# One FFN's input product in a two-layer FP32 kernel: eight block products per column pair replaced by seven (one level of Strassen's algorithm)

## The chip, the cores and the metric

The kernel runs as one program on one NeuronCore of a Trainium2 chip. Its time is the device time of one execution in microseconds (us). TensorE (PE in the profile) does the matmuls, with its weight loads listed apart as PEld; VectorE (DVE), ScalarE (ACT) and GpSimd (POOL) do elementwise work; SyncE (SP) issues the DMA loads.

## The reference, cut to what matters

Two layers work on 256 latent tokens and 256 context tokens of width 1024. Each layer is a SwiGLU FFN, a mixing part (attention and Fourier branch), and another FFN; the output is a final normalisation of the latent tokens. Everything is FP32.

```
def swiglu(u, w_in, w_out):
    a, b = jnp.split(u @ w_in, 2, axis=-1)
    return (jax.nn.silu(a) * b) @ w_out

def ffn_sublayer(x, m, i, g, w_in, w_out):
    u = modulate(rms_norm(x, g), m, i)
    return x + 0.5 * m[:, 3 * i + 2][:, None] * swiglu(u, w_in, w_out)
```

`w_in` is 1024 x 5632, so `u @ w_in` has 44 column blocks of 128: 22 of `a` and 22 of `b`. The change touches this input product in one place, the first FFN of the second layer (`l = 1`, `f = 0`), which works on both kinds of tokens.

## The kernel before, in words

Activations lie with features on the 128 partitions and tokens along the free dimension: 512 columns, the latent 256 (`LAT`) and then the context 256 (`CTX`). A feature dimension of 1024 is eight blocks `k` of 128. FP32 precision is had from a split: each operand is a rounded high part (type fp32r) and a low part, the difference, and each block product is three matmuls, high x high, high x low and low x high (`mm3`, lines 369 to 375).

Weights come in a fixed order as blocks of 128 x 1024, eight 128 x 128 tiles side by side. The class `Stream` loads them with one SP DMA each (`load_to`, line 176), and `split_pieces` (lines 180 to 194) makes the high part on ACT (line 192) and the low part on DVE or POOL (line 193, which engine is chosen by a pattern, here two on DVE, then one on POOL). `tiles` hands out the pieces and runs loads 6 and splits 2 blocks ahead.

All of this, the normalised input `u` (8 tiles), the gated products `g` (22 tiles, one for each pair) and the weight blocks, lives in one pool `slot` of 46 buffers of 4 KB per partition (line 223). A tile that gets a used buffer waits for the last reader of the tile before it. `tmp` has 7 buffers of 2 KB for short-lived values, and `psum` has 8 banks. Each engine runs its instructions in the order of the program text (`manual_schedule`, line 227); there is no reordering between them.

`ffn` (lines 597 to 673) works in pairs `j` of an `a` column block and the matching `b` block. The first two pairs run step by step with `u` as it becomes ready, latent tokens first (lines 636 to 657). The other twenty pairs run in the loop of lines 663 to 672: 8 blocks `k` x 3 matmuls of 512 columns into bank `pa`, the same into `pb`, and then `gated`: SiLU of `pa` on ACT (line 625), its product with `pb` on DVE (line 626), the high part of `g[j]` on ACT (line 627); `low` (line 631) puts the low part of `g[j]` on DVE.

Then `project_out` (lines 499 to 595) multiplies by `w_out`: for each of eight output blocks `m` it goes through `k = 0` to 21 in that order and needs `g[k]` at step `k`. `modulated` (lines 435 to 453) makes the next `u`; it runs at the end of the FFN before, one token kind after the other. PE does its matmuls in this order and doesn't pass one whose input is missing.

Of the kernel before, what the change touches and what calls it, by code (L numbers as in the profile page):

```python
# [11 lines left out]
F32 = mybir.dt.float32  # L12
# [6 lines left out]
P = 128  # L19
# [63 lines left out]


def ffn_in_order(first):
    order = []
    for k in range(KC):
        for j in range(first):
            order += [(k, j), (k, NF + j)]
    for j in range(first, NF):  # L90
        order += [(k, j) for k in range(KC)]
        order += [(k, NF + j) for k in range(KC)]
    return order
# [68 lines left out]
class Stream:  # L162
# [3 lines left out]
    def __init__(self, nc, pool, blocks):  # L166
        self.nc, self.pool, self.blocks = nc, pool, blocks
        self.raw, self.hl = {}, {}
        self.n_raw = self.n_split = 0
        self.pos = 0  # L170
        self.ahead, self.tick, self.lo_on = (6, 2), None, "v"

# [22 lines left out]

    def split_to(self, b):
        while self.n_split <= min(b, len(self.blocks) - 1):
            for _ in self.split_pieces(1):
                pass
# [20 lines left out]
def tile_kernel(ctx: ExitStack, tc, d, out):  # L220
# [135 lines left out]
    st = Stream(nc, slot, blocks)  # L356

# [5 lines left out]
    def cols(ss):  # L363
        return slice(S * ss[0], S * (ss[-1] + 1))
# [69 lines left out]

    def modulated(u, l, i, s, r):

        c = cols([s])

# [5 lines left out]
        for j in range(KC):  # L444
            t = temp("ut")
            nc.vector.scalar_tensor_tensor(out=t[:, c], in0=x[:, j, c], scalar=mod(l, 3 * i + 1, j, s), in1=r[:, c], op0=ALU.mult, op1=ALU.mult)
            nc.scalar.activation(u[j][:, 0, c], t[:, c], AF.Identity, bias=mod(l, 3 * i, j, s))
            if before:
                low(*before)
            before = j, t  # L450
            if j == KC - 1:
                low(*before)
            yield
# [143 lines left out]
    def ffn(l, f, ss, u, later, after):  # L597
# [34 lines left out]

        first = ffn_first(l, f)
        stagger = [[s] for s in ss] if first == 2 else [ss]
        w = []
        for n, part in enumerate(stagger):
# [5 lines left out]
            for k in range(KC) if first != START_PAIRS else ():  # L642
# [5 lines left out]
                if n == 0 and k == (E_K if e else 4) and later:  # L648
                    later()
                    later = None  # L650
            before = None
# [11 lines left out]
        for j in range(first, NF):  # L663
            pa, pb = bank("pa"), bank("pb")
            for ps in (pa, pb):
                tiles = st.tiles(8)
                for k in range(KC):
                    if len(ss) == 1:
                        mm_wide(ps, tiles[k], u[k], c, k == 0, k == KC - 1)
                    else:  # L670
                        mm3(ps[:, c], tiles[k], parts(u[k], c), k == 0, k == KC - 1)
            low(*gated(j, pa, pb, c))
        return project_out(l, i, ss, lambda k: g[k], NF, after, SILU if f else LN_EXP)
# [683 lines left out]
```

## Time and profile before

| | us |
|---|---|
| median of 3 runs | 2014.0 |
| lowest and highest | 2012.76, 2014.69 |
| the profiled execution: time | 2016.41 |
| its span, first to last instruction | 2014.5 |
| second layer, first FFN: pairs 2 to 21 | 1202.6 to 1420.2 |

In the rows below, a row of the groups of instructions reads "line engine operation output<-inputs, shape out<-in, count | busy time in all, mean ns of one | idle time of that engine just before them". A row of a tile's view gives minimum/median/maximum duration in ns. A row of the timeline reads "start, duration, engine, line, operation". A row of the stretches gives, after the stretch and its length, the busy time (and count) of PE, PEld, DVE, ACT and POOL, then the clock that TensorE was granted (1.00 is full), the DMA share and GB/s. Matmuls overlap in the pipeline, so the time that PE needs for them is read from the distance between starts, not from the duration of one.

### The profile page before, as it was taken

The page shows a single profiled execution, that of the slowest core. Times are in us where ns is not written, and L with a number is a line of the kernel's source. Part 1 is how long each engine was busy: PE and PEld are TensorE (multiplying, and loading weights), DVE is VectorE, ACT ScalarE, POOL GpSimd, SP SyncE. Part 2 cuts the span into 40 slices and gives each one's busy share as a digit, 9 for nine tenths or more (in the row PEclk, how much of TensorE's full clock was granted, in tenths as well). Part 3 has the DMA queues.
Part 4 walks back from the last instruction along what each step waited for, and adds up shares of the span by engine and source line. Part 5 has one row for each costly group of instructions (what it writes and reads, how often), then busy time and mean ns, then how long its engine had stood idle before and what let it go on. Part 6 is the DMA issues. An engine that isn't in the chain of part 4 may idle for free.

```text
span 2014.5 us, 26969 instructions
## 1 busy us (share of the span) xinstructions
PE 1992.3 (99%) x10388; PEld 1702.2 (84%) x10388; DVE 1211.7 (60%) x1832; ACT 823.0 (41%) x1335; POOL 735.6 (37%) x492
## 2 busy tenths in 40 slices
PE   8999999999999999999999999999999999999998
PEld 7888888888888888988888898888888889898887
DVE  5877786667777334677777252332324687776652
ACT  3432232256666323523223242222323565666661
POOL 0334455546553013243358410111222454224463
PEclk9999999999999999999999999999999999999999
DMA  9555565413222334455569332222421333555461
GB/s 378 204 169 176 167 210 210 165 58 110 92 85 93 105 105 137 157 172 173 178 212 353 104 131 82 91 74 84 139 91 53 126 128 119 192 172 193 158 203 59
DMA packets 86704, 297.58 MB, mean 148 GB/s; under 512 B 10032, under 2 KB 13232, under 8 KB 86576
## 3 DMA queue, kind: packets, MB, share of 16 engines
q1 hardware_dynamic: 86288, 295.34, 43.7%
q8 instruction: 81, 1.33, 0.3%
q10 hardware_dynamic: 288, 0.52, 0.1%
q14 instruction: 47, 0.39, 0.1%
HBM read 287.44 MB, written 1.05 MB: 143 GB/s over the span
## 4 chain that ended last, share of the span: by engine, by line
PE 93%; DVE 3%; ACT 2%; issue 1%; POOL 1%; DVEq 0%; POOLq 0%; ACTq 0%
PE po L375 7%; PE po L374 7%; PE po L373 7%; PE pa L373 5%; PE pb L375 5%; PE pa L375 5%; PE pb L373 5%; PE pa L374 5%; PE pb L374 5%; PE pg L373 2%; PE pg L375 2%; PE pg L374 2%; PE po L380 2%; PE pb L380 2%; PE pa L380 2%; PE pv L696 1%
## 5 line engine op out<-in xcount | busy, mean ns | idle before, releaser
L193 POOL TENSOR_TENSOR wlo<-wraw,whi 128x1024 fp32r<-128x1024 f32 x139 | 366.0, 2635 | 605.4 <-ACT whi L192 487.1
L192 ACT ACTIVATE whi<-wraw 128x1024 fp32r<-128x1024 f32 x392 | 395.5, 1049 | 74.8 <-PE po L374 34.1
L193 DVE TENSOR_TENSOR wlo<-wraw,whi 128x1024 fp32r<-128x1024 f32 x253 | 350.3, 1394 | 117.9 <-ACT whi L192 116.3
L302 DVE SCALAR_TENSOR_TENSOR junk<-mraw,cond 128x1024 bf16<-128x1024 f32 x224 | 303.1, 1395 | 1.1 <-DMA mraw<-in_w_mod 1.1
L373 PE MATMUL po<-g,whi 128*128 128x512 f32 (+1 forms) x616 | 223.8, 363 | 0.0
L375 PE MATMUL po<-g,wlo 128*128 128x512 f32 (+1 forms) x616 | 223.3, 362 | 0.0
L374 PE MATMUL po<-g,whi 128*128 128x512 f32 (+1 forms) x616 | 223.3, 362 | 0.0
L627 ACT ACTIVATE g<-gv 128x512 fp32r<-128x512 f32 (+1 forms) x92 | 51.7, 562 | 373.6 <-DVE gv L626 344.0
L317 POOL TENSOR_SCALAR mval<-macc,small 128x2 f32<-128x2 f32 (+1 forms) x88 | 122.3, 1394 | 216.2 <-DVE junk L302 216.2
L373 PE MATMUL pa<-u,whi 128*128 128x512 f32 x472 | 183.6, 389 | 0.0
L374 PE MATMUL pa<-u,whi 128*128 128x512 f32 x472 | 183.6, 389 | 0.0
L375 PE MATMUL pa<-u,wlo 128*128 128x512 f32 x472 | 183.6, 389 | 0.0
L373 PE MATMUL pb<-u,whi 128*128 128x512 f32 x472 | 183.6, 389 | 0.0
L374 PE MATMUL pb<-u,whi 128*128 128x512 f32 x472 | 183.6, 389 | 0.0
L375 PE MATMUL pb<-u,wlo 128*128 128x512 f32 x472 | 183.6, 389 | 0.0
L626 DVE TENSOR_TENSOR gv<-silu,pb 128x512 f32<-128x512 f32 x59 | 40.6, 688 | 182.3 <-PE pb L375 181.3
L462 DVE SCALAR_TENSOR_TENSOR x<-po,mval,x 128x256 f32<-128x256 f32 x73 | 32.6, 479 | 194.5 <-PE po L375 194.5
L374 PEld LDWEIGHTS po<-g,whi 128*128 128x128 f32 x616 | 116.3, 189 | 18.3
L373 PEld LDWEIGHTS po<-g,whi 128*128 128x128 f32 x616 | 116.2, 189 | 18.3
L375 PEld LDWEIGHTS po<-g,wlo 128*128 128x128 f32 x616 | 116.2, 189 | 17.9
L424 POOL TENSOR_TENSOR acc<-acc,sq 128x256 f32<-128x256 f32 (+1 forms) x46 | 53.2, 1156 | 191.5 <-ACT sq L413 191.5
L413 ACT ACTIVATE sq<-x 128x256 f32<-128x256 f32 (+1 forms) x48 | 24.7, 516 | 235.3 <-DVE x L462 202.8
(262 smaller groups left out, 4555.2 us busy)
## 6 DMA issues: line engine op xcount, KB each, us to landing
wraw<-in_ffn_in SPq DMA_DIRECT2D x176, 512.0 KB, 4.2
mraw<-in_w_mod SPq DMA_DIRECT2D x128, 512.0 KB, 3.7
wraw<-in_ffn_out SPq DMA_DIRECT2D x88, 512.0 KB, 4.4
wraw<-in_qk SPq DMA_DIRECT2D x32, 512.0 KB, 4.0
wraw<-in_g SPq DMA_DIRECT2D x32, 512.0 KB, 4.4
mfirst<-in_w_mod_first SPq DMA_DIRECT2D x16, 512.0 KB, 10.2
wraw<-in_v SPq DMA_DIRECT2D x16, 512.0 KB, 4.1
wraw<-in_attn SPq DMA_DIRECT2D x16, 512.0 KB, 4.0
```

The lines of the kernel that those rows point to most:

```text
L192: nc.scalar.activation(hi[:, c], raw[:, c], AF.Copy)
L193: eng.tensor_tensor(out=lo[:, c], in0=raw[:, c], in1=hi[:, c].bitcast(F32), op=ALU.subtract)
L302: nc.vector.scalar_tensor_tensor(out=tmp.tile([P, D], BF16, tag="t", name="junk"), in0=mod_raw[n], scalar=1.0, in1=cond[s], op0=ALU.mult, ...
L317: eng.tensor_scalar(out=o, in0=v, scalar1=b_mod[:, b:b + 1], scalar2=0.5 if i % 3 == 2 else 1.0, op0=ALU.add, op1=ALU.mult)
L373: nc.tensor.matmul(ps, hi, uh, start=first, stop=False)
L374: nc.tensor.matmul(ps, hi, ul, start=False, stop=False)
L375: nc.tensor.matmul(ps, lo, uh, start=False, stop=last)
L380: nc.tensor.matmul(ps.rearrange("p (a b) -> p a b", a=2), hi, t[:, :, c], start=first, stop=False)
L424: nc.gpsimd.tensor_tensor(out=self.acc[:, c], in0=self.acc[:, c], in1=sq[:, c], op=ALU.add)
L462: nc.vector.scalar_tensor_tensor(out=x[:, m, c], in0=ps[:, c], scalar=mod(l, 3 * i + 2, m, s), in1=x[:, m, c], op0=ALU.mult, op1=ALU.add)
L626: nc.vector.tensor_tensor(out=v[:, c], in0=sl[:, c], in1=pb[:, c], op=ALU.mult)
L627: nc.scalar.activation(g[j][:, 0, c], v[:, c], AF.Copy)
```

## The change

For pairs 4 to 21 of this one FFN the product of a pair is seen as a 2 x 2 by 2 x 2 block product: rows `a` and `b`, inner blocks `k` 0 to 3 and 4 to 7, columns latent and context. It is done with seven block products of 4 x 3 matmuls of 256 columns, where the eight of the plain form were done as 16 x 3 matmuls of 512. The seven need sums of weight blocks (`s1`, `s2`) and of input blocks (`tq`), and sums of the results.

- The packing order of the weights puts the four quarters of a pair into two blocks, `r0` and `r1`. These blocks are loaded, but not split, by `Stream` (`whole`, `take`).
- `modulated` also writes an unsplit copy of `u` (`full`, four slots) with one more ACT operation for each `k` and token kind.
- `sums` makes the four combinations of input blocks for one quarter index and splits them into two `tq` slots; it runs four times, twice during the first two pairs and twice in pair 2.
- `prepare` makes the seven split weight operands of a pair. It is a generator with five steps, run between the products of the pair before. `sevens` hands on the five steps of its first pair one by one, and yields again only at its own end.
- The gated products of pairs 10 to 21 are kept unsplit, two to a slot (`gf`), and split after the last pair.

```diff
-def ffn_in_order(first):
+SEVEN = {(1, 0): (4, 10)}
...
+    low, high = range(KC // 2), range(KC // 2, KC)
+    for j in range(seven, NF):
+        order += [(k, j) for k in low] + [(k, NF + j) for k in high]
+        order += [(k, NF + j) for k in low] + [(k, j) for k in high]
...
             nc.scalar.activation(u[j][:, 0, c], t[:, c], AF.Identity, bias=mod(l, 3 * i, j, s))
+            if keep:
+                q = j % (KC // 2)
+                if q not in full:
+                    full[q] = slot.tile([P, 4, S], F32, tag="s", name="uf")
+                nc.scalar.activation(full[q][:, 2 * (j // (KC // 2)) + s], t[:, c], AF.Identity, bias=mod(l, 3 * i, j, s))
...
+        def sums(q):
...
+            b = full.pop(q)
+            nc.vector.tensor_tensor(out=b[:, 0], in0=b[:, 0], in1=b[:, 1], op=ALU.subtract)
...
+            tq[q] = [slot.tile([P, 4, S], F32R, tag="s", name="tq") for _ in range(2)]
+            nc.scalar.activation(tq[q][0], b, AF.Copy)
+            nc.vector.tensor_tensor(out=tq[q][1], in0=b, in1=tq[q][0].bitcast(F32), op=ALU.subtract)
+
+        def sevens(j0, held_from):
...
+            def prepare(j, w):
...
+                r0, r1 = (st.take(block(j) + n) for n in range(2))
+                h0, l0 = (slot.tile([P, 1024], F32R, tag="s", name=n) for n in ("h0", "l0"))
+                nc.scalar.activation(h0, r0, AF.Copy)
+                s1 = slot.tile([P, 1024], F32, tag="s", name="s1")
+                for n in (one, two):
+                    nc.vector.tensor_tensor(out=s1[:, n], in0=r0[:, n], in1=r1[:, one], op=ALU.add)
+                nc.gpsimd.tensor_tensor(out=l0, in0=r0, in1=h0.bitcast(F32), op=ALU.subtract)
+                w["a11"], w["a22"] = ((h0[:, n], l0[:, n]) for n in (one, two))
+                yield
+                s2 = slot.tile([P, 1024], F32, tag="s", name="s2")
+                nc.vector.tensor_tensor(out=s2[:, one], in0=s1[:, two], in1=r0[:, one], op=ALU.add)
+                nc.vector.tensor_tensor(out=s2[:, two], in0=s2[:, one], in1=r1[:, two], op=ALU.add)
...
+                yield
+                a12 = slot.tile([P, 1024], F32R, tag="s", name="a12")
+                nc.scalar.activation(a12[:, one], r1[:, two], AF.Copy)
+                nc.vector.tensor_tensor(out=a12[:, two], in0=r1[:, two], in1=a12[:, one].bitcast(F32), op=ALU.subtract)
...
+                yield
...
+                nc.scalar.activation(h1, s1, AF.Copy)
+                nc.gpsimd.tensor_tensor(out=l1, in0=s1, in1=h1.bitcast(F32), op=ALU.subtract)
...
+                yield
...
+                nc.scalar.activation(h2, s2, AF.Copy)
+                nc.vector.tensor_tensor(out=l2, in0=s2, in1=h2.bitcast(F32), op=ALU.subtract)
...
+                yield
...
+            def result(j, v, sl):
+
+                nc.vector.tensor_tensor(out=v[:, :S], in0=ps2[j][:, :S], in1=v[:, :S], op=ALU.subtract)
+                ps2.pop(j)
+                if j < held_from:
+                    nc.vector.tensor_tensor(out=v, in0=sl, in1=v, op=ALU.mult)
+                    return
...
+                g[j] = held.pop(0)
+                nc.vector.tensor_tensor(out=g[j], in0=sl, in1=v, op=ALU.mult)
...
+            for _ in prepare(j0, ws[j0]):
+                yield
...
+            for j in range(j0, NF):
...
+                p1, ps2[j], p3 = bank("pone"), bank("ptwo"), bank("pthree")
+                v, sl = temp("gv"), temp("silu")
+                some(todo, 1)
+                product(p1, w, "a11", b11, True)
+                nc.scalar.activation(v[:, :S], p1[:, :S], AF.Copy)
+                some(todo, 1)
+                product(p3, w, "s1", t1, True)
+                nc.scalar.activation(v[:, S:], p3[:, :S], AF.Copy)
+                nc.gpsimd.tensor_tensor(out=v[:, S:], in0=v[:, S:], in1=v[:, :S], op=ALU.add)
+                some(todo, 1)
+                if before:
+                    i, vi, si = before
+                    product(ps2[i], ws.pop(i), "a22", t4, False)
+                    result(i, vi, si)
+                some(todo, 1)
+                product(ps2[j], w, "s2", t2, True)
+                nc.vector.tensor_tensor(out=sl[:, S:], in0=ps2[j][:, :S], in1=v[:, S:], op=ALU.subtract)
+                if before and i < held_from:
+                    parted(i, vi)
+                some(todo, 1)
+                product(p1, w, "a12", b21, False)
+                nc.scalar.activation(sl[:, :S], p1[:, :S], AF.Silu)
+                if before and i < held_from:
+                    low(g[i], slice(0, 512), vi)
+                product(p3, w, "s4", b22, False)
+                nc.vector.tensor_tensor(out=sl[:, S:], in0=p3[:, :S], in1=sl[:, S:], op=ALU.subtract)
+                nc.scalar.activation(sl[:, S:], sl[:, S:], AF.Silu)
+                st.load_to(block(j + 2) + 1)
+                product(ps2[j], w, "s3", t3, False)
+                nc.vector.tensor_tensor(out=v[:, S:], in0=ps2[j][:, :S], in1=v[:, S:], op=ALU.subtract)
+                before = j, v, sl
+                del p1, p3
+            st.split_to(st.pos + 1)
+            i, vi, si = before
+            product(ps2[i], ws.pop(i), "a22", t4, False)
+            result(i, vi, si)
+            tq.clear()
+            st.load_to(st.pos + 3)
+            for j in range(held_from, NF):
+                v = g[j]
+                parted(j, v)
+                low(g[j], slice(0, 512), v)
+            yield
...
-        for j in range(first, NF):
+        seven, held_from = SEVEN.get((l, f), (NF, NF))
+        more = sevens(seven, held_from) if seven < NF else iter(())
+        for j in range(first, seven):
...
+                if full:
+                    sums(min(full))
+                elif seven < NF:
+                    some(more, 3)
             low(*gated(j, pa, pb, c))
+        some(more, 100)
```

`product` is 4 x 3 matmuls of 256 columns, `parted` is the ACT copy that makes the high part of `g[j]`, `some(steps, n)` advances a generator `n` times, and `t1` to `t4` are the four quarters of the `tq` tiles.

More of the change, by code (lines that the diff above doesn't have):

```diff
@@ L79, with ffn_in_order @@
 STEPWISE = [[0, 3, 3, 1], [4, 2]]
-def ffn_in_order(first):
+SEVEN = {(1, 0): (4, 10)}
+def ffn_in_order(first, seven=NF):
     order = []
@@ L171, in __init__ @@
         self.ahead, self.tick, self.lo_on = (6, 2), None, "v"
+        self.whole, self.n_whole = set(), {}
     def load_to(self, b):
@@ L194, in split_pieces, with take @@
             yield
+    def take(self, b):
+        self.load_to(b)
+        return self.raw.pop(b)
     def split_to(self, b):
         while self.n_split <= min(b, len(self.blocks) - 1):
+            if self.n_split in self.whole:
+                self.n_split += 1
+                continue
             for _ in self.split_pieces(1):
@@ L356, in tile_kernel @@
     st = Stream(nc, slot, blocks)
+    per_layer = len(blocks) // DEPTH
+    for (l, f), (j, _) in SEVEN.items():
+        b = l * per_layer + (per_layer - 66 if f else 0)
+        st.whole |= set(range(b + 2 * j, b + 2 * NF))
+        st.n_whole[l, f] = b + 2 * j
     def tick():
@@ L433, in total @@
             return rsqrt(ps, D, c, "rinv")
+    full = {}
     def modulated(u, l, i, s, r):
         c = cols([s])
+        keep = i != 1 and (l, i // 2) in SEVEN
         def low(j, t):
@@ L650, in ffn @@
                     later = None
+                if n and k in (3, 7) and full:
+                    sums(min(full))
             before = None
@@ L662, in ffn @@
                 nc.scalar.activation(cond[n], cond[n], AF.Silu)
-        for j in range(first, NF):
+        seven, held_from = SEVEN.get((l, f), (NF, NF))
+        more = sevens(seven, held_from) if seven < NF else iter(())
+        for j in range(first, seven):
             pa, pb = bank("pa"), bank("pb")
-            for ps in (pa, pb):
+            for n, ps in enumerate((pa, pb)):
                 tiles = st.tiles(8)
@@ L671, in ffn @@
                         mm3(ps[:, c], tiles[k], parts(u[k], c), k == 0, k == KC - 1)
+                if full:
+                    sums(min(full))
+                elif seven < NF:
+                    some(more, 3)
             low(*gated(j, pa, pb, c))
+        some(more, 100)
         return project_out(l, i, ss, lambda k: g[k], NF, after, SILU if f else LN_EXP)
@@ L1335 @@
         for f in range(2):
[L1336 removed]
+            dr[f"ffn_in_{l}{f}"] = pack(a["ffn_w_in"][l, f], ffn_in_order(ffn_first(l, f), SEVEN.get((l, f), (NF,))[0]))
             dr[f"ffn_out_{l}{f}"] = pack(a["ffn_w_out"][l, f], FFN_OUT_ORDER)
```

48 lines of the change are left out of this document (47 added, 1 removed).

## The prediction

> **What bounds the kernel now.** I read the page first, then the busy time by stretches around the FFN that changes, then the durations of its groups, then single collisions in the timeline.
>
> ```profile
> span 2014.5 us, 26969 instructions
> PE 1992.3 (99%) x10388; PEld 1702.2 (84%) x10388; DVE 1211.7 (60%) x1832; ACT 823.0 (41%) x1335; POOL 735.6 (37%) x492
> ...
> PE 93%; DVE 3%; ACT 2%; issue 1%; POOL 1%; DVEq 0%; POOLq 0%; ACTq 0%
> ...
> 1203.00:1420.00 217.00, 217.00 (x959) 179.64 (x959) 67.97 (x68) 62.65 (x82) 31.79 (x13) 1.00 0.28 86
> 1420.00:1435.00 15.00, 15.00 (x68) 12.43 (x67) 7.36 (x4) 7.61 (x8) 5.37 (x2) 1.00 0.48 161
> ```
>
> PE is the bound. In the stretch of pairs 2 to 21, and at the start of `project_out` behind it, it has no idle time at full clock, while DVE works 68 of 217 us, ACT 63 and POOL 32. Fewer matmuls would pay here if nothing else fills up.
>
> ```profile
> L373 PE MATMUL pa<-u,whi x160: 389/389/396, 1202.6 to 1414.1; 128*128 128x512 f32 x160
> L375 PE MATMUL pb<-u,wlo x160: 389/389/389, 1208.5 to 1420.0; 128*128 128x512 f32 x160
> ...
> 1193.23 0.28 PE L373 MATMUL pf<-u,whi 128*128 128x256 f32 x1
> 1202.23 0.28 PE L373 MATMUL pf<-u,whi 128*128 128x256 f32 x1
> ```
>
> From 1202.6 to 1420.0 are 959 steps between 960 matmuls of 512 columns: 0.2267 us each. Between the two `pf` rows lie 75 steps of 256 columns: 0.120 us each, more than half of 0.2267. A pair costs 48 x 0.2267 = 10.88 us.
>
> **The change, term by term.**
>
> *PE.* A pair becomes 84 matmuls of 256 columns: 84 x 0.120 = 10.08 us, 0.80 us less. Eighteen pairs: **-14.4 us**, if PE stays the bound. The Trainium skill ("TensorE: Matmul & The Clock Gate", section "Back-to-back issue gap") gives N/2.4 + 2.5 ns for N columns, 216 and 109 ns; by it a pair would save 1.2 us and the change 21 us. The trace shows 11 ns more for both sizes, and the measurement decides.
>
> *Elementwise work.* In these pairs a weight block took one ACT copy and one subtraction; now sums, four splits, result sums and a longer way to `g` are needed.
>
> ```profile
> L193 DVE TENSOR_TENSOR wlo<-wraw,whi x23: 1216/1226/2630, 1216.1 to 1391.1; 128x1024 fp32r<-128x1024 f32 x23
> L193 POOL TENSOR_TENSOR wlo<-wraw,whi x11: 2394/2403/2537, 1227.1 to 1390.2; 128x1024 fp32r<-128x1024 f32 x11
> ...
> L192 ACT ACTIVATE whi<-wraw 128x1024 fp32r<-128x1024 f32 x40 | 39.8, 1044 | 0.0
> L631 DVE TENSOR_TENSOR g<-gv,g 128x512 fp32r<-128x512 f32 x19 | 13.2, 693 | 13.5 <-ACT g L627 13.5
> L627 ACT ACTIVATE g<-gv 128x512 fp32r<-128x512 f32 x19 | 12.0, 632 | 106.9 <-DVE gv L626 106.9
> ...
> L951 POOL TENSOR_TENSOR osqp<-osq,osqp 128x256 fp32r<-128x256 f32 x5 | 3.7, 736 | 0.4
> ...
> L386 DVE TENSOR_TENSOR silu<-pa,silu x20: 423/425/427, 1840.7 to 1940.9; 128x256 f32<-128x256 f32 x20
> ...
> L622 DVE TENSOR_TENSOR gv<-silu,gv x20: 425/910/966, 1842.3 to 1943.4; 128x256 f32<-128x256 f32 x20
> ...
> 1248.74 2.36 DVE L193 TENSOR_TENSOR wlo<-wraw,whi 128x1024 fp32r<-128x1024 f32 x2 [0.26 <-ACT whi L192]
> ```
>
> Two DVE operations back to back take 2.36 us, not 2 x 1.22: each overlaps the next by 0.08. So a subtraction of 1024 columns occupies DVE for 1.14 us, one of 512 for 0.61, one of 256 from PSUM for 0.34. A new pair has on DVE: two `s1`, two `s2`, the low part of `a12`, the product in `result` and `low`, seven of 512 with both inputs in SBUF (4.29), `l2` of 1024 (1.14), and four of 256 that read PSUM (1.38): **6.81 us**. POOL gets `l0` and `l1` (2.40 each) and one addition of 256 (0.74). ACT gets three copies of 1024, two of 512 and four of 256, about 6 us. Each alone fits under 10.08 us.
>
> *They don't run side by side.* This is what I weigh most:
>
> ```profile
> 1227.05 2.40 POOL L193 TENSOR_TENSOR wlo<-wraw,whi 128x1024 fp32r<-128x1024 f32 x1 [18.40 <-ACT whi L192]
> 1227.96 2.58 DVE L193 TENSOR_TENSOR wlo<-wraw,whi 128x1024 fp32r<-128x1024 f32 x1 [1.21 <-ACT whi L192]
> ...
> 1840.46 2.49 POOL L193 TENSOR_TENSOR wlo<-wraw,whi 128x1024 fp32r<-128x1024 f32 x1 [4.74 <-ACT whi L192]
> 1840.68 0.42 DVE L386 TENSOR_TENSOR silu<-pa,silu 128x256 f32<-128x256 f32 x1
> 1842.32 0.92 DVE L622 TENSOR_TENSOR gv<-silu,gv 128x256 f32<-128x256 f32 x1
> ```
>
> The DVE subtraction at 1227.96 takes 2.58 us for 1.23 us of work: it began at 1229.31, 0.14 before POOL's ended at 1229.45. At 1840 the operation that reads PSUM (`pa`) isn't slowed under POOL (0.42), the one with both inputs in SBUF is (0.92; 0.910 in the median, against 0.425 for the same size undisturbed). So a POOL operation and a DVE operation with two SBUF inputs exclude each other, each for its whole length, with a handover of 0.14. The Trainium skill says so ("SBUF — State Buffer", section "Who interferes with whom": the shared pair is an exclusive lock, and a DVE instruction with two SBUF inputs contends with a GpSimd one that reads SBUF); the trace agrees with 0.910 against 0.425. It is the rule that speaks against this change.
>
> A POOL turn costs DVE 2.40 - 0.14 = 2.26 us, the small one 0.60. Per pair the two engines then need 4.29 + 1.14 + 2 x 2.26 + 0.60 = **10.55 us** if one of them always holds the lock: a floor above PE's 10.08. The order of the program doesn't reach it. DVE's queue for a pair is: `s1`, `s1`, `s2`, `s2`, `a12` low, `result` (two), `sl`, `l2`, `low`, `sl`, `v`. POOL's `l0`, addition and `l1` become ready (ACT copies `h0`, `p3`, `h1`) while DVE is in the first four, so all three turns fall between DVE operations that wait for them, and the PSUM readers, which could run under POOL, stand behind in the queue. That makes 6.81 + 5.12 = 11.9 us. For pairs whose predecessor is below 10, `l2` also waits: it needs `h2` on ACT, which stands behind `parted`, which waits for the product in `result`: after that 0.54 + 1.04 + some 0.15 of handover, of which DVE fills 0.34 with `sl`. So 13.3 us. Without `parted` and `low` it is 11.9 - 0.6 + about 0.2 = 11.5.
>
> PE feels it at its seventh product (`s3`): it accumulates into the bank that DVE's first `sl` must have read, so PE idles there for what is over 10.08, 1.4 to 3.2 us each pair. PE can't get ahead, since the operands of the next pair come from the same queue.
>
> Six pairs (5 to 10) at 13.3 and twelve at 11.5 are 218 us. Slots: `u` 8, `tq` 8, `g` 10 and up to 5 `gf` leave 15 of 46, and a pair in flight uses up to 15. From about pair 16 on a tile waits for the last reader of one that has just come free: between 0 and 2 us for each of six pairs; I take 1. Loop: **224 us** against 18 x 10.88 = 195.8: **+28 us** (ends: 190 at the floor of 10.55, 240 if all pairs take 13.3).
>
> *The end of the loop.* In pair 3 the generator is advanced three times behind `pa` and three times behind `pb`. `prepare` gives five steps; the sixth call runs through the whole loop of eighteen pairs to the last `yield`. `gated` of pair 3 stands behind that call, so its SiLU, product, copy and `low` come behind the twelve `parted` and `low` of the held pairs on ACT and DVE. `project_out` needs `g[3]` at its fourth step, 3 x 0.68 = 2.0 us after it starts. DVE by then has, from PE's last product: 0.2 to arrive, 0.34 + 0.61, twelve times 0.61 = 7.3, then 0.69 + 0.63 + 0.69 and handovers: 10.7 us. PE stands for about **9 us** where it had no idle time before. A stall of that length also lowers the clock:
>
> ```profile
> 12.00:15.00 3.00, 1.25 (x9) 0.85 (x7) 1.95 (x3) 2.42 (x3) 0.00 (x0) 1.00 1.07 391
> 15.00:18.00 3.00, 2.70 (x15) 2.70 (x16) 2.86 (x4) 0.00 (x0) 0.00 (x0) 0.67 1.03 410
> ...
> 1173.00:1203.00 30.00, 29.69 (x240) 29.14 (x240) 21.12 (x41) 17.31 (x33) 3.20 (x2) 1.00 0.54 207
> ...
> L447 ACT ACTIVATE u<-ut,mval x16: 492/510/512, 1174.9 to 1195.4; 128x256 fp32r<-128x256 f32 x16
> ```
>
> A stretch in which PE worked 1.25 of 3 us is followed by one at 0.67, some 3.4 us at half clock: **+1.5 us**. Later steps of `project_out` are covered: `low` runs ahead of them.
>
> *Before the loop.* Sixteen more ACT copies of 0.51 us stand between those that the context products wait for (PE waited some 0.3 us there); four `sums` (DVE 2.5 us, ACT 1.0 each) lie beside pair 2's 10.9 us. Cover is nearly all there: 0 to 2 us, I take **+1**. The `tq` split and the raw loads, two blocks for each pair as before, hide under PE.
>
> *Sum:* 28 + 9 + 1.5 + 1 = +39.5. The profiled execution took 2016.4 (2 us around its span of 2014.5), the median is 2014.0; I add to the median: **2054 us**.
>
> **The rivals.**
>
> - *The lock packs.* DVE and POOL drift until one always holds it: 10.55 to 11 us a pair, the loop 190 to 198. With 11.5 for the ends: 2014 - 6 + 11.5 to 2014 + 2 + 11.5, so 2018 to 2038 with what lies between. For: the floor itself. Against: three POOL turns that DVE's order can't use.
> - *PE stays the bound, the end stalls:* -14.4 + 11.5 = -3, 2011 us. It needs collisions to be absorbed; the 20 rows of `L622` speak against it.
> - *PE stays the bound and the end doesn't stall* (the other side): `g[3]` finished before the held pairs, or the sums' collisions without price: 2014 - 14.4 + 1 = 2001 us. It decides if DVE and POOL together stay under 10.08 a pair.
> - *Worse:* every pair at 13.3, slots short: 240 + ends, 2070 us.
> - That the change doesn't do what it says: then PE's count would not rise by 18 x (84 - 48) = 648.
>
> **How the numbers follow.** Forecast, 2038 to 2070: 0.66. Packed, 2018 to 2038: 0.17. End stall alone, about 2011: 0.08. Faster, about 2001: 0.09. A measurement of this kernel can tell some 0.2%, 4 us, from no change. So faster 0.09, same 0.08, slower 0.83. Range: 2020 to 2070, leaving out the two cases at or below 2014 and the tail above.
>
> **What would show it.** In the profile after: PE count 11036; starts of the first products 11.5 to 13.3 us apart, with PE idle before the seventh product and DVE's first `sl` as its releaser; `s2` and the low part of `a12` with means far over 0.69 us; one PE wait of some 9 us before the fourth step of `project_out` with `low` (L631) as releaser, then a clock below 1. I am wrong if DVE's two-input operations show undisturbed means, if pairs stand 10.1 us apart, or if `g` of pair 3 is done before the held ones.

## The result, and the profile after

The changed kernel takes **2063.7 us** in the median (2061.77 to 2067.32, four runs), beside 2013.64 us for the kernel before on the same chip (2012.76 to 2014.69, four runs). The ratio is 1.025, with a 95% interval of 1.0233 to 1.0268: 2.5% slower, 50 us. The profiled execution took 2065.36 us, with a span of 2063.6.

One line of the diff above is miscopied: in the loop, the first `sl` line stands with `in1=v[:, S:]`. The program (line 789 after) has `in1=v[:, :S]`, so this instruction waits for ScalarE's copy of `p1` and not for GpSimd's addition. Line numbers from here on are those of the changed kernel: `wlo` is on L203, `prepare` on L692 to 725 (`s1` L699, `s2` L704 and 705, the low part of `a12` L710), the loop on L767 to 804. In the experiments a line can stand a few further down.

The head of the page and its chain, then the stretches (the columns are as before: busy time and count of PE, PEld, DVE, ACT and POOL, granted clock, DMA share, GB/s) around the changed loop and at the start of `project_out`:

```profile
span 2063.6 us, 28653 instructions
PE 1994.5 (97%) x11036; PEld 1733.2 (84%) x11036; DVE 1375.7 (67%) x2008; ACT 873.9 (42%) x1445; POOL 821.2 (40%) x534
PE 82%; DVE 12%; ACT 3%; issue 2%; POOL 1%; DMA 1%; SPq 0%; DVEq 0%; ACTq 0%; POOLq 0%
```

```profile
1225.00:1435.00 210.00, 176.97 (x1342) 171.63 (x1341) 192.03 (x189) 87.58 (x140) 109.28 (x50) 0.94 0.23 72
1465.00:1480.00 15.00, 8.28 (x25) 6.37 (x26) 12.55 (x13) 9.94 (x13) 5.29 (x2) 0.66 0.58 217
```

PE's count rose by 648, so the change does what it says, and PE's busy time is nearly what it was (1994.5 against 1992.3): the time was not spent in matmuls. In the loop PE works 177 of 210 us where it worked all of them, DVE 192. Over the whole chain DVE's share went from 3% to 12%. In which instructions, the groups of DVE and POOL in the loop tell (x18 is once a pair; mean ns behind the busy time):

```profile
L710 DVE TENSOR_TENSOR a<-wraw,a 128x512 fp32r<-128x512 f32 x18 | 47.5, 2637 | 0.0
L704 DVE TENSOR_TENSOR s<-s,wraw 128x512 f32<-128x512 f32 x18 | 39.6, 2200 | 0.8
L699 DVE TENSOR_TENSOR s<-wraw 128x512 f32<-128x512 f32 x36 | 34.2, 990 | 2.9 <-DMA wraw<-in_ffn_in 2.8
L722 DVE TENSOR_TENSOR l<-s,h 128x1024 fp32r<-128x1024 f32 x18 | 24.1, 1338 | 8.0 <-ACT h L721 8.0
L705 DVE TENSOR_TENSOR s<-s,wraw 128x512 f32<-128x512 f32 x18 | 19.7, 1097 | 0.6
L754 DVE TENSOR_TENSOR gf<-silu,gv 128x512 f32<-128x512 f32 x12 | 10.1, 838 | 0.5
...
L789 DVE TENSOR_TENSOR silu<-ptwo,gv 128x256 f32<-128x256 f32 x18 | 7.5, 417 | 0.3 <-PE ptwo L734 0.3
```

```profile
L732 PE MATMUL ptwo<-tq,h 128*128 128x256 f32 x216 | 65.3, 302 | 30.1 <-DVE silu L789 29.5 <-DVE gv L802 0.6
```

A subtraction of 512 columns takes 0.69 us undisturbed; here L710 takes 2.64 and L704 2.20 in the mean, while L789, which reads PSUM, keeps its 0.42. PE waits 29.5 us for that L789, at the seventh product. The timeline of one pair shows why L704 and L710 are long: each lasts until a POOL operation ends.

```profile
1250.19 2.82 POOL L700 TENSOR_TENSOR l<-wraw,h 128x1024 fp32r<-128x1024 f32 x1 [3.84 <-ACT h L696]
1252.98 1.18 POOL L781 TENSOR_TENSOR gv<-gv 128x256 f32<-128x256 f32 x1
1254.13 2.85 POOL L716 TENSOR_TENSOR l<-s,h 128x1024 fp32r<-128x1024 f32 x1
```

```profile
1250.77 2.79 DVE L704 TENSOR_TENSOR s<-s,wraw 128x512 f32<-128x512 f32 x1
1253.60 1.12 DVE L705 TENSOR_TENSOR s<-s,wraw 128x512 f32<-128x512 f32 x1
1254.63 2.89 DVE L710 TENSOR_TENSOR a<-wraw,a 128x512 fp32r<-128x512 f32 x1
```

POOL's `l0` ends at 1253.01 and L704 at 1253.56, 0.55 us later; POOL's `l1` ends at 1256.98 and L710 at 1257.52. Between the two, POOL's addition and L705 take their turns in the same way.

And in `project_out`, the wait at its fourth step, with the clock that follows (a matmul of 512 columns every 0.43 us where it was 0.23):

```profile
1471.72 0.79 PE L396 MATMUL po<-g,whi 128*128 128x512 f32 x1 [8.12 <-ACT g L658]
...
1473.04 0.63 PE L398 MATMUL po<-g,wlo 128*128 128x512 f32 x1
1473.46 0.63 PE L396 MATMUL po<-g,whi 128*128 128x512 f32 x1
1473.89 0.63 PE L397 MATMUL po<-g,whi 128*128 128x512 f32 x1
```

Comparing the starts of the same matmuls in the two profiled executions gives the account of the 49.1 us between the spans:

| where | us |
|---|---|
| in the program's first 31 us, in which both kernels do the same | +1.9 |
| from there to the first pair of seven (its start at 1224.38 becomes 1230.29, 5.9 later in all) | +4.0 |
| loop of 18 pairs: 195.84 becomes 231.08 | +35.2 |
| start of `project_out` to a point late in its eighth block, behind the norm's first two matmuls: 115.75 becomes 126.70 | +11.0 |
| given back behind it, nearly all in the last FFN | -3.0 |

### The profile page after: what moved, and what is told of

Its sections match the earlier page's. It is cut to its first block, busy times and chain, and to the rows that moved or that the text cites. A ratio compares the mean times of both kernels' runs of the same rounds, so it can differ in the third digit from the quotient of the medians.

```text
span 2063.6 us, 28653 instructions
## 1 busy us (share of the span) xinstructions
PE 1994.5 (97%) x11036; PEld 1733.2 (84%) x11036; DVE 1375.7 (67%) x2008; ACT 873.9 (42%) x1445; POOL 821.2 (40%) x534
## 4 chain that ended last, share of the span: by engine, by line
PE 82%; DVE 12%; ACT 3%; issue 2%; POOL 1%; DMA 1%; SPq 0%; DVEq 0%; ACTq 0%; POOLq 0%
PE po L396 7%; PE po L398 7%; PE po L397 7%; PE pa L396 3%; PE pb L396 3%; PE pa L397 3%; PE pb L397 3%; PE pa L398 3%; PE pb L398 3%; DVE a L710 2%; PE pg L396 2%; PE pg L397 2%; PE pg L398 2%; DVE s L704 2%; PE po L403 2%
## 5 line engine op out<-in xcount | busy, mean ns | idle before, releaser
L203 POOL TENSOR_TENSOR wlo<-wraw,whi 128x1024 fp32r<-128x1024 f32 x127 | 337.6, 2660 | 455.5 <-ACT whi L202 380.7
L202 ACT ACTIVATE whi<-wraw 128x1024 fp32r<-128x1024 f32 x356 | 359.6, 1049 | 74.7 <-PE po L397 29.7
L203 DVE TENSOR_TENSOR wlo<-wraw,whi 128x1024 fp32r<-128x1024 f32 x229 | 313.9, 1379 | 108.1 <-ACT whi L202 104.2
L658 ACT ACTIVATE g<-gv 128x512 fp32r<-128x512 f32 (+1 forms) x74 | 40.4, 545 | 269.2 <-DVE gv L657 237.5
L398 PE MATMUL pb<-u,wlo 128*128 128x512 f32 x328 | 127.7, 389 | 0.6 <-POOL wlo L203 0.6
L398 PE MATMUL pa<-u,wlo 128*128 128x512 f32 x328 | 127.7, 389 | 0.5 <-DVE wlo L203 0.5
L396 PE MATMUL pa<-u,whi 128*128 128x512 f32 x328 | 127.7, 389 | 0.0
L397 PE MATMUL pa<-u,whi 128*128 128x512 f32 x328 | 127.6, 389 | 0.0
L397 PE MATMUL pb<-u,whi 128*128 128x512 f32 x328 | 127.6, 389 | 0.0
L396 PE MATMUL pb<-u,whi 128*128 128x512 f32 x328 | 127.6, 389 | 0.0
L732 PE MATMUL ptwo<-tq,h 128*128 128x256 f32 x216 | 65.3, 302 | 30.1 <-DVE silu L789 29.5
```

The lines of the kernel that those rows point to most:

```text
L202: nc.scalar.activation(hi[:, c], raw[:, c], AF.Copy)
L203: eng.tensor_tensor(out=lo[:, c], in0=raw[:, c], in1=hi[:, c].bitcast(F32), op=ALU.subtract)
L396: nc.tensor.matmul(ps, hi, uh, start=first, stop=False)
L397: nc.tensor.matmul(ps, hi, ul, start=False, stop=False)
L398: nc.tensor.matmul(ps, lo, uh, start=False, stop=last)
L732: nc.tensor.matmul(ps[:, :S], hi[:, k], bh, start=first and q == 0, stop=False, skip_group_check=True)
```

## The experiments

The theory was that of the prediction: turns of POOL and DVE at the memory make a pair 11.5 to 13.3 us long, `gated` of pair 3 stalls the projection, and, seen in the trace after, DVE comes into the loop with a backlog. The rival to the first: the pairs are long because of the order of DVE's queue, the slots or the waits for POOL's results, whatever the memory does.

**The gate ahead of the loop.**

```diff
-                    some(more, 3)
+                    some(more, 3 - n)
```

> Only the last step's call is cut from three steps to two where it is made the second time (`some(more, 3 - n)`), so that the gate of pair 3 is issued ahead of the loop and not behind it; nothing else is moved. My theory of the end (the gate of pair 3 stands behind the twelve held pieces, and TensorE waits 8.51 us for it at the fourth step of the projection): that wait goes, and with it the lower clock behind it; 10.95 us were measured from the start of the projection to its m = 7, so the time falls by 8 to 11 us, to 2053 to 2056. Rival (the projection is late because the slots and the held pieces are late, whatever the gate does): the wait moves to a later step of the projection, and the time stays at 2061 or more. The loop itself keeps its 231 us by both, give or take 2.

Measured: 2060.81 us (ratio to before 1.0238, 1.0223 to 1.0253), 3 us less, where 8 to 11 were expected: it lies between the two ranges, just under the rival's. By the ratios it is 2.4 us less, with intervals that overlap, so what the edit did is read from the traces. The wait of 8.12 us is gone, as the same stretch of `project_out` shows, which here has full clock. A shorter one stands later in that stretch, for a weight's low part that GpSimd makes:

```profile
1465.00:1480.00 15.00, 13.00 (x58) 10.47 (x58) 11.30 (x17) 12.57 (x18) 8.38 (x2) 1.00 0.77 286
...
1478.59 0.50 PE L398 MATMUL po<-g,wlo 128*128 128x512 f32 x1 [2.00 <-POOL wlo L203]
```

That is the rival's kind of move, at a quarter of the size. From its start to the same point in the eighth block the projection takes 118.10 us, 8.6 less. But the loop takes 235.93, 4.85 more, against "give or take 2". Of that 1.6 us come in the first eight pairs, where the gate now stands ahead of the first pair's parts on DVE, and 3.2 in pairs 16 to 20. A gate made before the loop holds a slot all through it, and the loop was short of slots at its end already; a late transfer moves DVE's operations against POOL's turns:

```profile
1389.61 4.04 DVE L699 TENSOR_TENSOR s<-wraw 128x512 f32<-128x512 f32 x2 [1.29 <-DMA wraw<-in_ffn_in]
```

So the mechanism of the end is as predicted, and removing it moved some of the cost elsewhere. That a slot is the reason is argued here; the runs on held pairs below bear on it.

**GpSimd's three operations on VectorE.**

```diff
-                nc.gpsimd.tensor_tensor(out=l0, in0=r0, in1=h0.bitcast(F32), op=ALU.subtract)
+                nc.vector.tensor_tensor(out=l0, in0=r0, in1=h0.bitcast(F32), op=ALU.subtract)
...
-                nc.gpsimd.tensor_tensor(out=l1, in0=s1, in1=h1.bitcast(F32), op=ALU.subtract)
+                nc.vector.tensor_tensor(out=l1, in0=s1, in1=h1.bitcast(F32), op=ALU.subtract)
...
-                nc.gpsimd.tensor_tensor(out=v[:, S:], in0=v[:, S:], in1=v[:, :S], op=ALU.add)
+                nc.vector.tensor_tensor(out=v[:, S:], in0=v[:, S:], in1=v[:, :S], op=ALU.add)
```

> The three operations that GpSimd has in a pair (`l0`, `l1` and the addition in `v`) are given to VectorE; the order of each queue, the slots and the products stay. My theory (GpSimd and VectorE take turns at the memory that they share, so that GpSimd's time comes on top of VectorE's): VectorE then has 6.81 + 2 x 1.15 + 0.32 = 9.43 us in a pair, less than the 10.08 us of the products; the pairs stand 10.1 to 11 us apart in place of 11.7 to 14.5, the loop takes 190 to 200 us in place of 231, and the total is 2020 to 2034 with the wait at the end still there. Rival (the pair is long because VectorE's own queue is long or because its order holds it, and GpSimd's work lies beside it): VectorE gets 2.6 us more in every pair and the loop gets longer, by up to 17 x 2.6 = 44 us, for 2064 to 2108.

Measured: 2024.6 us (1.0058, 1.0043 to 1.0073), 39 us less than the change, with *more* work on the busiest elementwise engine. The rival's range begins 39 us higher. The groups of DVE, and a stretch of the loop:

```profile
L704 DVE TENSOR_TENSOR s<-s,wraw 128x512 f32<-128x512 f32 x18 | 12.3, 686 | 0.0
L710 DVE TENSOR_TENSOR a<-wraw,a 128x512 fp32r<-128x512 f32 x18 | 12.3, 685 | 0.0
```

```profile
1244.00:1375.00 131.00, 131.00 (x1092) 130.81 (x1091) 120.98 (x188) 67.19 (x111) 0.00 (x0) 1.00 0.31 97
```

L704 and L710 are back at 0.69 us, PE has no idle time from 1244 to 1375, and twelve pairs in a row stand 10.08 us apart, which is the prediction's 84 x 0.120. DVE is busy 121 of 131 us and that suffices. The loop takes 189.8 us; the wait in the projection is still there, 8.20 us.

**Turns, or waits for results?** The first run gives GpSimd reads whose results nobody uses, the second writes alone; both start from the kernel with everything on VectorE.

```diff
+    spare = const.tile([P, 384], BF16, name="spare")
...
+                for n in (slice(0, 384), slice(384, 768)):
+                    nc.gpsimd.tensor_tensor(out=spare, in0=r0[:, n], in1=h0[:, n].bitcast(F32), op=ALU.subtract)
...
+                for n in (slice(0, 384), slice(384, 768)):
+                    nc.gpsimd.tensor_tensor(out=spare, in0=s1[:, n], in1=h1[:, n].bitcast(F32), op=ALU.subtract)
...
+                nc.gpsimd.tensor_tensor(out=spare[:, :S], in0=v[:, S:], in1=v[:, :S], op=ALU.add)
                 nc.vector.tensor_tensor(out=v[:, S:], in0=v[:, S:], in1=v[:, :S], op=ALU.add)
```

> VectorE keeps all of a pair's work, as in the run without GpSimd (2024.6 us), and GpSimd gets five operations a pair at the old places whose results nobody reads: four subtractions 128x384 of `r0`, `h0` and of `s1`, `h1`, and the addition of the halves of `v`, written to a spare tile. So no product and no other operation waits for a result of GpSimd, while it reads two operands again. My theory (turns at the memory): some 4 x 0.9 + 0.6 = 4.2 us of GpSimd's turns come on top of VectorE's 5.43 + 2.62 = 8.05 us with two operands in SBUF, with the handovers 12.9 us a pair at least: the pairs stand 12.9 to 14.5 us apart and the total is 2072 to 2100. Rival (the loop was long because work waited for GpSimd's results, which take 2.9 us each, and not because of turns): nothing waits for them now, so the pairs stay at 10.1 and the total is 2020 to 2030.

Measured: 2082.1 us (one run), inside the theory's range, 57 us over the kernel without GpSimd and even over the change. From the second on, pairs stand 12.65 to 14.40 us apart. DVE's operations are long again (three lines stand ahead of them, so L707 is the first `s2` and L713 the low part of `a12`): against their means without GpSimd they take 58 us more in the loop. One wait for GpSimd was left in after all (the addition in place must wait until GpSimd has read `v`), 7.5 us over the loop, far too little for 57:

```profile
L707 DVE TENSOR_TENSOR s<-s,wraw 128x512 f32<-128x512 f32 x18 | 24.4, 1353 | 0.0
L713 DVE TENSOR_TENSOR a<-wraw,a 128x512 fp32r<-128x512 f32 x18 | 23.8, 1322 | 0.0
...
L787 DVE TENSOR_TENSOR gv<-gv 128x256 f32<-128x256 f32 x18 | 15.8, 877 | 7.5 <-POOL spare L786 7.5
```

```diff
                 nc.vector.tensor_tensor(out=s2[:, two], in0=s2[:, one], in1=r1[:, two], op=ALU.add)
+                nc.gpsimd.memset(r0, 0.0)
...
+                nc.gpsimd.memset(r1, 0.0)
...
+                nc.gpsimd.memset(s1, 0.0)
...
+                nc.gpsimd.memset(s2, 0.0)
```

> As the run without GpSimd (2024.6 us), and GpSimd clears `r0`, `r1`, `s1` and `s2` in each pair behind their last reader (four memsets of 128 x 1024, some 1 us each by the nearest row, 64x512 in 0.52 us): it only writes. The Trainium skill, page SBUF - State Buffer, section Who interferes with whom, says that a VectorE instruction with two operands in SBUF contends with a GpSimd instruction that reads SBUF, not with one that only writes it. By that rule the pairs stay at 10.1 to 10.6 us and the total is 2022 to 2034. Rival (any work of GpSimd takes the turn): 4.2 us of turns come on top, the pairs stand 12.5 to 14 us apart, total 2065 to 2095.

Measured: 2032.88 us (one run). GpSimd is busy 68.7 us in the loop, and DVE doesn't feel it:

```profile
L706 POOL MEMSET wraw<- 128x1024 f32 x18 | 17.2, 956 | 77.6 <-DVE s L704 60.4 <-ACT h L717 9.1 <-ACT a L710 8.1
```

```profile
L699 DVE TENSOR_TENSOR s<-wraw 128x512 f32<-128x512 f32 x36 | 23.2, 686 | 9.8 <-DMA wraw<-in_ffn_in 9.8
...
L704 DVE TENSOR_TENSOR s<-s,wraw 128x512 f32<-128x512 f32 x18 | 12.3, 686 | 0.0
L711 DVE TENSOR_TENSOR a<-wraw,a 128x512 fp32r<-128x512 f32 x18 | 12.3, 685 | 0.0
```

The means are 0.686 and 0.685 us, to the nanosecond those without GpSimd. The rule of the Trainium skill ("SBUF — State Buffer", section "Who interferes with whom": a VectorE instruction with two SBUF inputs contends with a GpSimd instruction that reads SBUF, not with one that only writes it) agrees with these two runs. Of the 8 us over the run without GpSimd 5.8 stand in the loop, nearly all of them late, where pairs stretch to 10.5 to 14.3 us and DVE waits 9.8 us for transfers instead of 5.3. That a buffer is free only when GpSimd has cleared it is the likely reason; it is argued. Another 3.0 us stand in the last FFN, which the edit doesn't touch (see the last section).

**Start later.** With the gate ahead of the loop, and GpSimd as in the change:

```diff
-SEVEN = {(1, 0): (4, 10)}
+SEVEN = {(1, 0): (6, 10)}
...
-                    some(more, 3)
+                    some(more, 3 if (j, n) == (3, 0) else 2 if (j, n) == (3, 1) else 0)
```

> The seven products begin two pairs later (`SEVEN` (6, 10)), and the gate of pair 3 is issued ahead of the loop as in the run before last: pairs 4 and 5 are made with eight products, in which VectorE can work off the four `sums` that stood ahead of the first pair's parts. My theory of the start (the first pair's parts are late because VectorE comes with a backlog: 18.55 us for the first pair in place of some 11.7, and three to four us ahead of it): the first pair of seven is then 11.5 to 13 us long and the start comes without a wait; two pairs with eight products cost 10.9 us each in place of 12 to 14. So 7 to 12 us less than with the gate alone: 2042 to 2049. Rival (the first pair is long whatever comes before, since its parts are made in line and not one pair ahead): the first pair stays at 17 us or more and the time is within 4 us of that with the gate alone, 2049 to 2056.

Measured: 2054.06 us (1.0203, 1.0188 to 1.0219), 6.75 less than with the gate alone. The time is above the range given and inside the rival's, since both stood on a gate that saves 10; the gain is just short of the 7 to 12 expected. The first pair takes 13.53 us in place of 21.57, where the rival said 17 or more. But the edit did two things: it put two plain pairs behind the `sums`, and it had the first pair's parts made two pairs ahead of their use and no longer just before it. So it doesn't tell a backlog on DVE from parts made in line. For the backlog speak the plain pairs, which were late too: PE waits 3.06 us for a weight split on DVE there.

**All three together.** The two lines of the run just shown, and the three operations on VectorE.

```diff
-SEVEN = {(1, 0): (4, 10)}
+SEVEN = {(1, 0): (6, 10)}
...
-                nc.gpsimd.tensor_tensor(out=l0, in0=r0, in1=h0.bitcast(F32), op=ALU.subtract)
+                nc.vector.tensor_tensor(out=l0, in0=r0, in1=h0.bitcast(F32), op=ALU.subtract)
...
-                    some(more, 3)
+                    some(more, 3 if (j, n) == (3, 0) else 2 if (j, n) == (3, 1) else 0)
```

> All three edits together: GpSimd's operations on VectorE, the gate ahead of the loop, the first pair of seven two pairs later. My theory (turns at the memory, backlog at the start, gate at the end, and nothing else of size): 14 or 15 pairs at 10.1 to 10.5 us where the kernel before has 10.88, no stall at the end, so that the loop with its two plain pairs takes 188 to 196 us against the 195.8 of before, and the total is 2004 to 2016 against 2013.6: from 0.5% faster to the same. Rival (a fourth term that all three leave in place, the slots or ScalarE's share): 2020 or more.

Measured: 2016.92 us (1.0022, 1.0013 to 1.0032): just over the theory's range, below the rival's. The trace names three rests: four of the last five distances are 11.07 to 11.53 us, PE waits 2.06 us for a weight split on GpSimd early in the projection, and pairs 3 to 5 take some 5 us more than 10.88 each, with PE waiting for weight splits that come late behind the `sums`.

**Backlog mended, fewer pairs held.**

```diff
-SEVEN = {(1, 0): (6, 10)}
+SEVEN = {(1, 0): (6, 14)}
...
-            nc.vector.tensor_tensor(out=tq[q][1], in0=b, in1=tq[q][0].bitcast(F32), op=ALU.subtract)
+            late.append((q, b))
+            while late and (late[0][0] != q or not full):
+                p, b = late.pop(0)
+                nc.vector.tensor_tensor(out=tq[p][1], in0=b, in1=tq[p][0].bitcast(F32), op=ALU.subtract)
...
-                    some(more, 3 if (j, n) == (3, 0) else 2 if (j, n) == (3, 1) else 0)
+                    some(more, 3 if (j, n) == (4, 0) else 2 if (j, n) == (4, 1) else 0)
```

> As the run with all three edits (2016.92 us), with three more: pairs 6 to 13 are split as they come and 14 to 21 held (`SEVEN` (6, 14), where 10 and on were held), the parts of the first pair of seven are prepared in the halves of pair 4 and not of pair 3, and in `sums` the low part of one quarter is issued behind the subtractions of the next, so that VectorE doesn't wait 1.13 us for ScalarE in each. My theory: of the run with all three, the last five pairs were 1 to 1.5 us over 10.08 for want of slots (about 5 us), the projection began with 2.45 us of waiting, and pairs 3 and 4 lost some 5 us to VectorE's backlog; most of the first two and about half of the third go, so 2006 to 2012, that is 0.1 to 0.3% faster than the kernel before. Rival (VectorE at 9.43 us a pair and 0.68 more for each pair that isn't held is itself the bound): the pairs up to 13 slip by 0.3 to 1 us each and the time stays at 2014 to 2020.

Measured: 2016.89 us (1.001, 1.0001 to 1.0019). By the ratios that is 0.1% less than the run before, with intervals that overlap: no gain that is clear of the spread. The rival's range holds the time, but not for the rival's reason: the pairs up to 13 stand 10.07 to 10.08 us apart. PE no longer waits anywhere from pair 2 to the first pair of seven, nor at the projection. All of that was given back at the end of the loop: pairs 14 to 20 stand 10.70 to 14.23 us apart, DVE undisturbed but waiting 11.6 us for transfers (three lines were added, so L702 is the sums `s1`, and L713 below the low part of `a12`):

```profile
L702 DVE TENSOR_TENSOR s<-wraw 128x512 f32<-128x512 f32 x12 | 7.8, 688 | 11.6 <-DMA wraw<-in_ffn_in 11.6
```

A gate that is split at once takes a whole slot, a held one half. Splitting four more pairs at once took two more slots, and the reading is that the transfers for the next pair wait for a free one. If so, the edit went the wrong way, and points at what to do.

**Every pair held.** From the run just shown:

```diff
-SEVEN = {(1, 0): (6, 14)}
+SEVEN = {(1, 0): (5, 5)}
...
-            for j in range(held_from, NF):
+            st.lo_on = "v"
+
+            def split_held(j):
                 v = g[j]
                 parted(j, v)
                 low(g[j], slice(0, 512), v)
+
+            for j in range(held_from, held_from + 6):
+                split_held(j)
+            rest.extend((split_held, j) for j in range(held_from + 6, NF))
...
-        return project_out(l, i, ss, lambda k: g[k], NF, after, SILU if f else LN_EXP)
+        def gate(k):
+            while rest:
+                do, j = rest.pop(0)
+                do(j)
+            return g[k]
+
+        return project_out(l, i, ss, gate, NF, after, SILU if f else LN_EXP)
```

> As the tuned run before (2016.89 us), but seven products from pair 5 on and every one of them held (`SEVEN` (5, 5)), so that a pair keeps half a slot of its gate and not a whole one; of the held pieces six are split ahead of the projection and the other eleven behind the splits of its first weights, which are VectorE's alone there. In the tuned run pairs up to 13 stood 10.08 us apart and the last seven 10.7 to 14.2, with VectorE and ScalarE waiting for a weight's transfer that had no free slot. My theory (slots are what the last pairs wait for; with all held there are 5 + 9 = 14 in use at the end where there were 18): 17 pairs at 10.08 to 10.2 us, no stall at the projection, so 17 x 0.8 - 3 = 10.6 us less than before, 2002 to 2007: faster by 0.3 to 0.55%. Rival (the last pairs are held up by the transfers themselves, whatever slots there are): they stay at 11 us or more and the time is 2009 or more; second rival (seventeen held pieces at the end delay the projection by more than a microsecond each few steps): the loop is short and the projection 5 us or more longer, 2008 to 2013.

Measured: **2006.69 us**, beside 2015.09 for the kernel before in the same session: ratio 0.9961, 0.9948 to 0.9973. This version beats both kernels. Its chain, its stretches from pair 2 into the eighth block of the projection, and the sums `s1` in its loop:

```profile
PE 92%; DVE 3%; ACT 2%; issue 1%; POOL 1%; DMA 0%; SPq 0%; DVEq 0%; ACTq 0%; POOLq 0%
```

```profile
1203.00:1235.00 32.00, 32.00 (x142) 26.48 (x142) 27.05 (x38) 15.73 (x21) 2.52 (x1) 1.00 0.12 33
1235.00:1409.00 174.00, 172.36 (x1432) 171.84 (x1431) 149.02 (x232) 84.04 (x137) 0.00 (x0) 1.00 0.32 104
1409.00:1527.00 118.00, 116.39 (x558) 97.96 (x557) 49.98 (x57) 35.11 (x48) 9.70 (x7) 1.00 0.33 100
...
L702 DVE TENSOR_TENSOR s<-wraw 128x512 f32<-128x512 f32 x32 | 20.6, 685 | 0.8 <-DMA wraw<-in_ffn_in 0.8
```

PE has no idle time ahead of the loop, 1.6 us in it and 1.6 behind it. All 16 distances are 10.01 to 10.08 us, the last pairs among them, and DVE waits 0.8 us for transfers: both rivals fall. Holding every pair also spares DVE and ACT a split in the loop, but in the run before pairs that were split at once stood 10.08 apart as well; so the two runs together show the slots as the term of the last pairs. In the profiled executions 17 pairs take 173.5 us where 17 x 10.88 = 185.0 were, -11.5; the projection +1.9; together -9.6, which is the difference of the spans (2004.9 against 2014.5).

**The same with GpSimd.** The three operations go back to GpSimd, and nothing else.

```diff
-                nc.vector.tensor_tensor(out=l0, in0=r0, in1=h0.bitcast(F32), op=ALU.subtract)
+                nc.gpsimd.tensor_tensor(out=l0, in0=r0, in1=h0.bitcast(F32), op=ALU.subtract)
...
-                nc.vector.tensor_tensor(out=l1, in0=s1, in1=h1.bitcast(F32), op=ALU.subtract)
+                nc.gpsimd.tensor_tensor(out=l1, in0=s1, in1=h1.bitcast(F32), op=ALU.subtract)
...
-                nc.vector.tensor_tensor(out=v[:, S:], in0=v[:, S:], in1=v[:, :S], op=ALU.add)
+                nc.gpsimd.tensor_tensor(out=v[:, S:], in0=v[:, S:], in1=v[:, :S], op=ALU.add)
```

> As the run it goes with (every pair held, start and end mended), but with the change's three operations a pair back on GpSimd, so that it tells what their place alone costs when everything else is mended. My theory (turns at the memory set 11.65 us a pair where no gate is split in the loop, as the change's pairs 12 to 15 stood): 17 x (11.65 - 10.08) = 27 us more than its partner, 2028 to 2036. Rival (start, slots and end were the trouble, and GpSimd's place matters only beside them): within 6 us of its partner.

Measured: 2034.69 us (1.01, 1.0085 to 1.0116), 28.0 more than its partner, where 27 were worked out. Of the sixteen distances ten are 11.67 us.

```profile
L713 DVE TENSOR_TENSOR a<-wraw,a 128x512 fp32r<-128x512 f32 x16 | 41.8, 2615 | 0.0
L707 DVE TENSOR_TENSOR s<-s,wraw 128x512 f32<-128x512 f32 x16 | 35.7, 2229 | 0.7
L702 DVE TENSOR_TENSOR s<-wraw 128x512 f32<-128x512 f32 x32 | 31.6, 1028 | 0.2
```

With start, end and slots mended, the place of three operations is the whole difference between 0.4% faster and 1.0% slower than before.

## Why the prediction was right, point by point

Predicted were 2054 us and slower, in a range of 2020 to 2070; 2063.7 lie in it. The terms were meant against the profiled execution, so its account is set beside them. The terms of the loop and of the end came out by their mechanisms; the one at the start was too small.

- **PE, 10.08 us a pair:** right, and visible only once DVE keeps up (twelve pairs in a row without GpSimd). In the change itself PE was not the bound, as forecast.
- **Turns at the memory:** right, and shown by three comparisons: work moved to DVE (-39 us), reads without use (+57), the move back (+28). The predicted price of POOL's turns was 5.12 us a pair. What DVE's operations L699, L704, L705, L710, L722 and L754 took over their means in the run without GpSimd adds up to some 84 us, 4.7 a pair.
- **The order of the queue:** 13.3 us were forecast for pairs 5 to 10 and 11.5 for the others. Measured were 13.13 in the mean of those six, and 11.72 for pairs 12 to 17. PE's starts alternate there (11.67 to 12.19 and 13.76 to 14.54), but DVE's own turn, from one L789 to the next, is 13.25 to 13.38 us in each of the six and 11.65 to 11.68 in most of the later ones. The 8.0 us that L722 waited for ACT's `h2` came in six waits, one a pair, as the step on `parted` said. The rival "the lock packs" gave 10.55 to 11 us a pair; none of the 17 distances is under 11.06.
- **Slots:** 6 us were forecast from pair 16 on; pairs 18 to 20 took 38.2 us, 3 more than at 11.72. In the change itself only DVE's 2.8 us of waiting for transfers point at the slots; the runs on held pairs show them for the kernel with everything on VectorE.
- **The end:** 9 us of wait and 1.5 of clock were forecast; 8.51 us lie between the start of the waiting matmul and that of the one before it, and 11.0 were lost in all. The clock cost more than forecast: the eleven distances from the waiting matmul on take 5.09 us, where 11 x 0.227 are 2.5, so 2.6 us. PE was released by ACT's `g` (L658), a step ahead of `low` (L662), which the prediction had named.
- **Before the loop and its first pair, the mis-sized term:** "Cover is nearly all there: 0 to 2 us, I take **+1**." It cost 4.0 us ahead of the loop and some 7 in its first pair, 18.55 us where 11.5 stood in the sum. That accounts for nearly all of the 10 us by which the forecast (+39.5) fell short of the three middle rows of the account (+50). The step set the `sums` against PE's time in pair 2, as work beside work. It didn't follow DVE's queue:

```profile
1221.63 2.61 DVE L670 TENSOR_TENSOR uf<-uf 128x256 f32<-128x256 f32 x1
...
1226.74 1.23 DVE L676 TENSOR_TENSOR tq<-uf,tq 128x1024 fp32r<-128x1024 f32 x1 [1.13 <-ACT tq L675]
1227.88 0.68 DVE L657 TENSOR_TENSOR gv<-silu,pb 128x512 f32<-128x512 f32 x1
1229.32 0.69 DVE L662 TENSOR_TENSOR g<-gv,g 128x512 fp32r<-128x512 f32 x1 [0.76 <-ACT g L658]
1229.93 3.44 DVE L699 TENSOR_TENSOR s<-wraw 128x512 f32<-128x512 f32 x2
```

Each of the `sums` waits 1.13 us for ACT in the middle, one lost 2.2 us to a POOL turn, and the first sum of the loop's first pair (L699) begins at 1229.93, when PE is about to want that pair's operands. They are made one after another while PE waits:

```profile
1230.29 0.39 PE L732 MATMUL pone<-u,h 128*128 128x256 f32 x1 [1.00 <-ACT h L696]
1232.88 0.39 PE L734 MATMUL pone<-u,l 128*128 128x256 f32 x1 [2.08 <-POOL l L700]
1237.10 0.58 PE L734 MATMUL pthree<-tq,l 128*128 128x256 f32 x1 [1.79 <-POOL l L716]
```

So the step left out that DVE comes late: the parts of the first pair, which stand in the program behind the first half of pair 3 (that half ends at 1222.84), are begun only when pair 3 is over. GpSimd's place adds to it, since without GpSimd the first pair took 13.93 us; and whether half a pair would have been time enough for the parts without the backlog, no run shows. How the 7 us divide is open. With the low parts deferred and the preparation one pair ahead the same work cost PE no wait from pair 2 to the loop.

## What to carry to other kernels

Before work is spread over GpSimd and VectorE, count what each reads from SBUF: VectorE alone, busy 9.3 of 10.08 us a pair, was faster than the two sharing the work, and GpSimd left VectorE's operations at their length only where it didn't read. Fewer matmuls pay only as far as the slowest elementwise queue allows, and that queue is to be followed at the loop's first and last turn, not only in its middle. An edit that removes a wait can also take a slot or a place in a queue that was covering another: the gate moved ahead gained 8.6 us at the end of the loop and gave 4.85 of it back inside.

## What the runs showed of the hardware that was not expected

**Clock inside the loop.** The prediction had the clock fall only at the long stall. In the change's loop it was 0.94: 0.66 in the first 15 us, where the first pair's waits follow one another, and 0.97 from there on, since the 3 us waits at the seventh product lower it too:

```profile
1272.33 0.58 PE L732 MATMUL ptwo<-tq,h 128*128 128x256 f32 x1 [3.01 <-DVE silu L789]
1272.70 0.41 PE L733 MATMUL ptwo<-tq,h 128*128 128x256 f32 x1
1272.92 0.41 PE L734 MATMUL ptwo<-tq,l 128*128 128x256 f32 x1
...
1275.05 0.41 PE L732 MATMUL pone<-u,h 128*128 128x256 f32 x1
```

Behind this wait of 3.01 us twelve distances in a row are 0.213 us, in place of 0.120; behind the waits of 1.34 us in the last run (its clock in the loop is 0.99) only the first distance is longer, 0.22, and the rest are 0.11 to 0.13. The Trainium skill ("TensorE: Matmul & The Clock Gate", section "Back-to-back issue gap") gives N/1.2 ns between matmuls of N columns for the cold array. An estimate from it for 256 columns is 213 ns, which is the distance measured here. As DVE set the pace, this added little to the mean of the pairs.

**An untouched stretch with two speeds.** The last FFN of the second layer, with PE at work all the time and the clock at 1.00, took 109.4 us from the first to the last of its 160 `pa` matmuls of this form in the change and 111.2 in the kernel before and in the fastest version:

```profile
L380 PE MATMUL pa<-u,whi x160: 391/398/495, 1828.0 to 1939.2; 128*128 128x512 f32 x160
```

```profile
L403 PE MATMUL pa<-u,whi x160: 391/391/501, 1880.1 to 1989.5; 128*128 128x512 f32 x160
```

The matmuls of the two kernels are the same there (512 and 256 columns in turn); their distances are 0.230 and 0.117 us in the median in the change, 0.236 and 0.118 before. This, 1.8 us, and the same in the projection behind it make up the 3.0 us given back in the account. Of the eleven profiled executions six have the shorter sum, 0.347 or 0.348 us (the change, the gate alone, no GpSimd, the late start, all three, the unneeded reads), and five the longer one, 0.353 or 0.354. The clock over the span doesn't sort them (0.998 with all three and with every pair held), and neither does GpSimd's work. Why is open.
